# Values and scores of one half as one ranked group of products on TensorE, in a two-layer hybrid decoder step

## Chip, cores and metric

The kernel runs on one core of one Trainium2 chip, as one program. The metric is the device time of one execution in microseconds (us). TensorE is called PE here (its weight loads PEld), VectorE DVE, ScalarE ACT, GpSimd POOL; SP is the engine that issues most of the DMAs. Line numbers (L286) are those of the kernel before.

## What is computed

One inference step of a two-layer decoder trunk, for a prompt of 256 tokens and for 8 samples of 8 new tokens each, all in fp32, 320 tokens together. Each layer is

```
x += 0.5 * SwiGLU(RMSNorm(x))
x += W_out [HGRN2 | RWKV-7 | MLA](RMSNorm(x) @ W_in)
x += 0.5 * SwiGLU(RMSNorm(x))
```

The part that matters here is the MLA attention of the samples over 2048 cached positions (16 pages of 128) of a paged cache. With 8 heads and 8 new tokens a sample has 64 rows of queries:

```
s_past = einsum('bqhr,bkr->bhqk', q_lat, c_past) + einsum('bqhe,bke->bhqk', q_pe, kpe_past)
s = concat([s_past * MLA_SCALE, s_new (causal)], -1)
pr = softmax(s)
o_lat = einsum('bhqk,bkr->bqhr', pr[..., :P], c_past) + einsum('bhqk,bkr->bqhr', pr[..., P:], c)
o = einsum('bqhr,rhd->bqhd', o_lat, wuv)
```

## The kernel before

Each layer is a feed-forward block, a mixer, and a second feed-forward block. In the feed-forward blocks PE runs dense products alone: a weight block of 128x128 is split by ACT and DVE (L427, L428) into a high and a low part, and each block takes part in three products with 320 columns.

In the mixer (L555) several streams of work are interleaved. They are Python generators, and `weave` (L518) advances them by a modelled PE time `self.pe`: a stream yields how much later it wants to be called again, and the first one that is due goes on. The first stage weaves the RWKV chain (`rw`), the samples' attention (`sample`), the dense products that fill (`rw_in`, `hg_in`) and a small split stream; the second stage weaves the HGRN chain (`hg`), the prompt's attention (`prompt`), the rest of `sample` and a part of the output projection (`w_out`). This fixes the order in which instructions are written down, not yet the order on the engines: a scheduler then gives each engine, whenever it is free in a simulated time line, the ready instruction of lowest rank. The rank is the place in the written order; `tc.high_priority(offset=n)` moves it n places ahead. The streams in `self.urgent` (RWKV, HGRN, prompt) have 1000 (L530). `tc.issue_after(ins)` puts an instruction behind another one on the same engine. On the chip each engine runs its order as it stands and waits where something is missing.

`sample` (L830) takes the samples in four pairs, p = 0 to 3. Sample si of a pair (0 or 1) uses output rows 64*si to 64*si + 63, so its products have 64 stationary columns, in one half of PE's columns. The pages of a sample are taken in four chunks (ch) of 512 positions, each of two halves (hf) of 256 positions, which are two pages.

- `scores(p, ch)` (L860): for each half the transposed keys of both samples are loaded (tile `ct`, 5 buffers, one DMA a page, L874), then 3 x 2 products of 96 rows by 256 columns go into a bank of PSUM (`pa`, 2 banks; L878). Each carries on from `kt` to the next. After both halves ACT copies the bank to `S` (L884), and DVE takes the maximum (L885).
- `soft(p)` (L887) adds the scores of the new tokens and makes the negative maximum for the exponential.
- `values(p, ch, po)` (L905): the natural pages of both samples are loaded (tile `cn`, 5 buffers, one DMA a page, L917), ACT takes the exponential of the next chunk (`exps`, L903), PE transposes this chunk's `S` in four products (L925, recorded under the helper's L290), DVE copies them to `PT` (L927), and then each half has 2 pages x 2 samples of products with 256 columns (L933), which accumulate in the bank `po` (tag `pv`, one bank) over the whole pair.
- The main loop (L944) runs, for each pair, `values(p, ch)` and then `scores(p + 1, ch)` for each chunk, so the next pair's scores are made beside this pair's values. At a pair's end come the new tokens' values, the normalisation and the transposed result (L951 to L974).

All products go through `mm` (L283, recorded as L286), transposes through `tr` (L289). `ready(name, n)` (L845) gives the modelled time at which the next loads will have landed, from a pace of 1.05 us a page and from when buffers were used. `pages` (L851) reads page numbers from the table into registers of SP. Each scores product and each values product is fp32 and appears in the trace as two matmul records.

Of the kernel before, what the change touches and what calls it, by code (L numbers as in the profile page):

```python
# [26 lines left out]
RANK = 256  # L27
# [4 lines left out]
NPOOL = 160  # L32
PAGE = 128
NPAGE = 16
# [16 lines left out]
KR = 96  # L51
# [205 lines left out]
class Kern:  # L257
# [572 lines left out]
    def sample(self):  # L830
        nc, l = self.nc, self.l
        self.mark(f"sample{l}")
        idt = self.c("ident")
        cT = self.cT
        cns = self.s([64, RANK], "cns")
        ps = self.bank("pa")
# [4 lines left out]
        S, mx = {}, {}  # L841
# [3 lines left out]
        def ready(name, n):  # L845
            f = feed[name]
            f[0] = max(f[0], f[1][f[2] - 3] if f[2] > 2 else 0.0) + n * (PACE[1] if f[2] < PACE[0] else 1.05)
            f[2] += 1
            return 0, f[0] + 2.2

        def pages(i, n):  # L851

            with self.tc.issue_after(self.gat[-8].ins) if len(self.gat) >= 8 else ExitStack():
                return nc.values_load_multi_w_load_instructions(  # L854
                    self.pti[0:1, i:i + n], engines=[mybir.EngineType.SP], min_val=0, max_val=NPOOL - 1,
                    skip_runtime_bounds_check_because="a page table names pages of the pool")[1]

        ctp = self.ap["ct"].rearrange("(n p) c -> n p c", p=KR)

        def scores(p, ch):  # L860
            ps = self.bank("pa")
            for hf in range(2):
                yield ready("ct", 4)
                self.mark(f"sample{l}")
                cts = []
                for si in range(2):
                    ct = self.s([KR, 2, 3 * PAGE], "ct", 5)
                    i0 = (2 * p + si) * NPAGE + ch * 4 + hf * 2
                    rs = pages(i0, 2)

                    n = 6 + 2 * (4 * ch + 2 * hf + si)
                    with self.tc.issue_after(self.raws[n]) if p == 0 and n < len(self.raws) else ExitStack():
                        for pg, r in enumerate(rs):
                            self.gat.append(nc.sync.dma_start(ct[:, pg, :], ctp[bass.ds(r + l * NPOOL, 1)].rearrange("a p c -> p (a c)")))  # L874
                    cts.append(ct)
                for kt in range(3):
                    for si in range(2):
                        self.mm(ps[64 * si:64 * si + 64, hf * 256:hf * 256 + 256], qlat[:KR, kt, 2 * p + si],  # L878
                                cts[si][:, :, kt * PAGE:kt * PAGE + PAGE], start=kt == 0, stop=kt == 2)
                feed["ct"][1].append(self.pe)  # L880
            S[p, ch] = self.s([128, 512], "S", 5)
            if ch == 0:
                mx[p] = self.s([128, 8], "smx", 2)
            nc.scalar.copy(S[p, ch], ps)  # L884
            nc.vector.tensor_reduce(out=mx[p][:, ch:ch + 1], in_=S[p, ch], axis=AX.X, op=ALU.max)  # L885
# [16 lines left out]
            m = mx[p]  # L902
            nc.scalar.activation(S[p, ch], S[p, ch], AF.Exp, bias=m[:, 5:6], scale=MLA_SCALE, accum_out=m[:, ch:ch + 1])  # L903

        def values(p, ch, po):  # L905
            r0 = ready("cn", 4)
            cns_ = []
            rs = []
            for si in range(2):
                i = (2 * p + si) * NPAGE + ch * 4  # L910
                rs.append(pages(i, 4))
            for hf in range(2):
                for si in range(2):
                    cn = self.s([128, 2, RANK], "cn", 5)
                    for pg in range(2):
                        r = rs[si][hf * 2 + pg]
                        self.gat.append(nc.sync.dma_start(cn[:, pg, :], self.ap["cn"][l, bass.ds(r, 1)].rearrange("a p c -> p (a c)")))  # L917
                    cns_.append(cn)
            yield 0, r0[1] - 1.5
            self.mark(f"sample{l}")  # L920
            if ch < 3:
                exps(p, ch + 1)
            pt = self.bank("pa")
            for pg in range(4):
                self.tr(pt[:, pg * 128:pg * 128 + 128], S[p, ch][:, pg * 128:pg * 128 + 128], idt)  # L925
            PT = self.s([128, 512], "PT", 2)
            nc.vector.tensor_copy(PT, pt)  # L927
            yield 0, max(self.pe + 1.2, r0[1])
            for hf in range(2):
                self.mark(f"sample{l}")  # L930
                for pg in (2 * hf, 2 * hf + 1):
                    for si in range(2):
                        self.mm(po[64 * si:64 * si + 64, :RANK], PT[:, pg * 128 + 64 * si:pg * 128 + 64 * si + 64],  # L933
                                cns_[2 * hf + si][:, pg % 2, :], start=ch == 0 and pg == 0, stop=False)
                feed["cn"][1].append(self.pe)
                if hf == 0:
                    yield ready("cn", 4)

        for ch in range(4):
            yield from scores(0, ch)  # L940
        yield 0
        soft(0)
        yield 2.0
        for p in range(4):  # L944
            po = self.bank("pv")
            exps(p, 0)
            for ch in range(4):
                yield from values(p, ch, po)
                if p < 3:
                    yield from scores(p + 1, ch)  # L950
            exps(p, 4)  # L951
            nc.vector.tensor_reduce(out=mx[p][:, 6:7], in_=mx[p][:, 0:5], axis=AX.X, op=ALU.add)
            nc.vector.reciprocal(mx[p][:, 6:7], mx[p][:, 6:7])
# [581 lines left out]
```

## Time and profile before

| what | value |
|---|---|
| median of 3 runs | 1675.93 us (1675.06 to 1678.35) |
| the profiled execution, its own time | 1670.47 us |
| its span from first to last instruction | 1668.5 us |
| PE, DVE, ACT, POOL busy | 1625.2, 955.0, 716.6, 80.2 us |
| matmul records on PE | 13174 |
| granted TensorE clock, mean | 0.988 of full speed |
| DMA | 260.05 MB, 156 GB/s in the mean |

The profile is one execution, so its times are set against its own 1670.47 us. A busy time is the union of an engine's instructions; PE's records are pipelined and overlap their successors, so the time that a run of products takes is read from its start to the start of what follows it. The idle time in brackets on a timeline row lies before that row, with what ended it.

### The profile page before, as it was taken

The page shows a single profiled execution, that of the slowest core. Times are in us where ns is not written, and L with a number is a line of the kernel's source. Part 1 is how long each engine was busy: PE and PEld are TensorE (multiplying, and loading weights), DVE is VectorE, ACT ScalarE, POOL GpSimd, SP SyncE. Part 2 cuts the span into 40 slices and gives each one's busy share as a digit, 9 for nine tenths or more (in the row PEclk, how much of TensorE's full clock was granted, in tenths as well). Part 3 has the DMA queues.
Part 4 walks back from the last instruction along what each step waited for, and adds up shares of the span by engine and source line. Part 5 has one row for each costly group of instructions (what it writes and reads, how often), then busy time and mean ns, then how long its engine had stood idle before and what let it go on. Part 6 is the DMA issues. An engine that isn't in the chain of part 4 may idle for free.

```text
span 1668.5 us, 33401 instructions
## 1 busy us (share of the span) xinstructions
PE 1625.2 (97%) x13174; PEld 1449.8 (87%) x13174; DVE 955.0 (57%) x1599; ACT 716.6 (43%) x1208; POOL 80.2 (5%) x112
## 2 busy tenths in 40 slices
PE   8999999999989899999999999999999999999998
PEld 8999998777657599999999999987766676999997
DVE  7555447854446585554465554478335565755543
ACT  6444334633343364443344443346233543544432
POOL 0000000200022000000000000002000310000000
PEclk9999999999999999999999999999999999999999
DMA  8555526646564465555545555366357644555442
GB/s 282 152 150 147 149 86 170 184 143 180 155 209 138 133 209 152 152 152 149 148 146 152 152 151 148 105 175 189 109 157 208 189 134 132 159 152 150 149 148 91
DMA packets 130908, 260.05 MB, mean 156 GB/s; under 512 B 17264, under 2 KB 75952, under 8 KB 130624
## 3 DMA queue, kind: packets, MB, share of 16 engines
q1 hardware_dynamic: 119072, 237.21, 48.0%
q10 hardware_dynamic: 11648, 20.65, 4.1%
q8 instruction: 104, 1.70, 0.4%
q0 software_dynamic: 32, 0.07, 0.1%
q14 instruction: 52, 0.43, 0.1%
HBM read 253.39 MB, written 4.47 MB: 155 GB/s over the span
## 4 chain that ended last, share of the span: by engine, by line
PE 65%; DVE 2%; DMA 2%; ACT 1%; SPq 1%; issue 1%; DVEq 0%; ACTq 0%
PE pd L286 25%; PE pr L286 23%; PE pa L286 14%; PE pv L286 3%; PE pa L290 1%; DMA cn<-in_cn 1%; ACT S L903 0%; DMA ct<-in_ct 0%; DVE w L428 0%; DMA raw<-in_wm 0%; SPq L874 0%; PE pd L290 0%; SPq L917 0%; SPq L854 0%; ACT L903 0%
## 5 line engine op out<-in xcount | busy, mean ns | idle before, releaser
L428 DVE TENSOR_TENSOR w<-raw,w 128x1024 fp32r<-128x1024 f32 (+1 forms) x392 | 410.9, 1051 | 321.4 <-ACT w L427 308.9
L427 ACT CAST w<-raw 128x1024 fp32r<-128x1024 f32 (+1 forms) x392 | 354.7, 909 | 425.0 <-PE pd L286 203.1
L286 PE MATMUL pd<-xh,w 128*128 128x320 f32 x1792 | 425.2, 316 | 7.7 <-ACT w L427 6.8
L286 PEld LDWEIGHTS pd<-xh,w 128*128 128x128 f32 x1792 | 305.6, 190 | 24.2 <-issue 9.7
L286 PE MATMUL pd<-xl,w 128*128 128x320 f32 x896 | 280.1, 314 | 0.0
L286 PE MATMUL pr<-xh,w 128*128 128x320 f32 x1056 | 240.2, 310 | 0.0
L286 PE MATMUL pa<-xh,w 128*128 128x320 f32 x896 | 201.7, 309 | 0.0
L286 PEld LDWEIGHTS pr<-xh,w 128*128 128x128 f32 x1056 | 178.3, 188 | 0.5
L286 PEld LDWEIGHTS pd<-xl,w 128*128 128x128 f32 x896 | 169.7, 189 | 2.9 <-issue 0.9
L286 PE MATMUL pr<-xl,w 128*128 128x320 f32 x528 | 162.5, 309 | 0.0
L286 PE MATMUL pd<-hh,w 128*128 128x320 f32 x704 | 158.2, 309 | 0.0
L286 PE MATMUL pr<-hh,w 128*128 128x320 f32 x704 | 158.2, 309 | 0.0
L286 PEld LDWEIGHTS pa<-xh,w 128*128 128x128 f32 x896 | 151.0, 188 | 0.0
L286 PE MATMUL pa<-xl,w 128*128 128x320 f32 x448 | 137.6, 309 | 0.0
L286 PE MATMUL pa<-ct,qlat 96*64 96x256 f32 x768 | 125.1, 398 | 3.9 <-DMA ct<-in_ct 3.9
L286 PEld LDWEIGHTS pr<-hh,w 128*128 128x128 f32 x704 | 118.5, 188 | 0.0
L286 PEld LDWEIGHTS pd<-hh,w 128*128 128x128 f32 x704 | 118.5, 188 | 0.0
L286 PE MATMUL pd<-hl,w 128*128 128x320 f32 x352 | 108.8, 309 | 0.0
L286 PE MATMUL pr<-hl,w 128*128 128x320 f32 x352 | 108.8, 309 | 0.0
L286 PEld LDWEIGHTS pr<-xl,w 128*128 128x128 f32 x528 | 99.1, 188 | 0.3
L475 ACT ACTIVATE fa<-fa 128x320 f32<-128x320 f32 x88 | 41.4, 472 | 134.7 <-DVE fa L474 134.7
L286 PEld LDWEIGHTS pa<-ct,qlat 96*64 96x64 f32 x768 | 59.2, 139 | 40.5 <-issue 13.5
(381 smaller groups left out, 2011.0 us busy)
## 6 DMA issues: line engine op xcount, KB each, us to landing
raw<-in_wf SPq DMA_DIRECT2D x264, 512.0 KB, 3.6
ct<-in_ct SPq DMA_DIRECT2D x256, 144.0 KB, 2.8
cn<-in_cn SPq DMA_DIRECT2D x256, 128.0 KB, 2.4
raw<-in_wm ACTq DMA_DIRECT2D x76, 256.0 KB, 3.3
raw<-in_wm SPq DMA_DIRECT2D x52, 256.0 KB, 3.7
xT<-in_x SPq DMA_DIRECT2D x4, 320.0 KB, 6.7
wukt<-in_wukt SPq DMA_DIRECT2D x2, 576.0 KB, 6.1
S<-in_rws SPq DMA_DIRECT2D x4, 256.0 KB, 3.4
```

Of the source, the lines that this page charges most:

```text
L286: self.last = self.nc.tensor.matmul(out, w, x, start=start, stop=stop)
L290: self.nc.tensor.transpose(out, x, ident)
L427: self.cast = nc.scalar.copy(h, src).ins
L428: nc.vector.tensor_tensor(out=lo, in0=src, in1=h.bitcast(F32), op=ALU.subtract)
L475: nc.scalar.activation(a, a, AF.Silu)
```

## The change

For a half of a chunk, the products of `values` and those of `scores` for the next pair now stand together. `scores` is cut into `keys` (the loads), `scores` (the products, with a rank 2000 ahead) and `scored` (copy and maximum). `values` becomes `chunk`: it asks for the loads of both halves first, keys and values in turn; then for each half it writes the four values products (2000 ahead), page 1 before page 0 and sample 1 before sample 0, and behind them, by `issue_after` on the last of them, the six scores products, sample 1 before sample 0. The transposes of the next chunk (`turned`, 2000 ahead) are placed behind the last product of the second half; those of a pair's chunk 0 stand before its first group. Pair 0's scores and pair 3's values have no partner and stand alone, with the same rank. The time at which a half is due is the later of the two streams' times. `exps`, `soft`, the copies and the end of a pair keep their rank.

```diff
--- before.py
+++ after.py
@@ -857,27 +857,38 @@
 
         ctp = self.ap["ct"].rearrange("(n p) c -> n p c", p=KR)
 
-        def scores(p, ch):
-            ps = self.bank("pa")
-            for hf in range(2):
-                yield ready("ct", 4)
-                self.mark(f"sample{l}")
-                cts = []
-                for si in range(2):
-                    ct = self.s([KR, 2, 3 * PAGE], "ct", 5)
-                    i0 = (2 * p + si) * NPAGE + ch * 4 + hf * 2
-                    rs = pages(i0, 2)
-
-                    n = 6 + 2 * (4 * ch + 2 * hf + si)
-                    with self.tc.issue_after(self.raws[n]) if p == 0 and n < len(self.raws) else ExitStack():
-                        for pg, r in enumerate(rs):
-                            self.gat.append(nc.sync.dma_start(ct[:, pg, :], ctp[bass.ds(r + l * NPOOL, 1)].rearrange("a p c -> p (a c)")))
-                    cts.append(ct)
+        def keys(p, ch, hf):
+
+            cts = []
+            for si in range(2):
+                ct = self.s([KR, 2, 3 * PAGE], "ct", 5)
+                rs = pages((2 * p + si) * NPAGE + ch * 4 + hf * 2, 2)
+
+                n = 6 + 2 * (4 * ch + 2 * hf + si)
+                with self.tc.issue_after(self.raws[n]) if p == 0 and n < len(self.raws) else ExitStack():
+                    for pg, r in enumerate(rs):
+                        self.gat.append(nc.sync.dma_start(ct[:, pg, :], ctp[bass.ds(r + l * NPOOL, 1)].rearrange("a p c -> p (a c)")))
+                cts.append(ct)
+            return cts
+
+        def latents(p, ch, hf):
+            cns_ = []
+            for si in range(2):
+                cn = self.s([128, 2, RANK], "cn", 5)
+                for pg, r in enumerate(pages((2 * p + si) * NPAGE + ch * 4 + hf * 2, 2)):
+                    self.gat.append(nc.sync.dma_start(cn[:, pg, :], self.ap["cn"][l, bass.ds(r, 1)].rearrange("a p c -> p (a c)")))
+                cns_.append(cn)
+            return cns_
+
+        def scores(p, hf, ps, cts):
+            with self.tc.high_priority(offset=2000):
                 for kt in range(3):
-                    for si in range(2):
+                    for si in (1, 0):
                         self.mm(ps[64 * si:64 * si + 64, hf * 256:hf * 256 + 256], qlat[:KR, kt, 2 * p + si],
                                 cts[si][:, :, kt * PAGE:kt * PAGE + PAGE], start=kt == 0, stop=kt == 2)
-                feed["ct"][1].append(self.pe)
+            feed["ct"][1].append(self.pe)
+
+        def scored(p, ch, ps):
             S[p, ch] = self.s([128, 512], "S", 5)
             if ch == 0:
                 mx[p] = self.s([128, 8], "smx", 2)
@@ -902,42 +913,60 @@
             m = mx[p]
             nc.scalar.activation(S[p, ch], S[p, ch], AF.Exp, bias=m[:, 5:6], scale=MLA_SCALE, accum_out=m[:, ch:ch + 1])
 
-        def values(p, ch, po):
-            r0 = ready("cn", 4)
-            cns_ = []
-            rs = []
-            for si in range(2):
-                i = (2 * p + si) * NPAGE + ch * 4
-                rs.append(pages(i, 4))
-            for hf in range(2):
-                for si in range(2):
-                    cn = self.s([128, 2, RANK], "cn", 5)
-                    for pg in range(2):
-                        r = rs[si][hf * 2 + pg]
-                        self.gat.append(nc.sync.dma_start(cn[:, pg, :], self.ap["cn"][l, bass.ds(r, 1)].rearrange("a p c -> p (a c)")))
-                    cns_.append(cn)
-            yield 0, r0[1] - 1.5
+        def turned(p, ch):
+
+            pt = self.bank("pa")
+            with self.tc.high_priority(offset=2000):
+                for pg in range(4):
+                    self.tr(pt[:, pg * 128:pg * 128 + 128], S[p, ch][:, pg * 128:pg * 128 + 128], idt)
+            self.PT = self.s([128, 512], "PT", 2)
+            nc.vector.tensor_copy(self.PT, pt)
+
+        def chunk(p, ch, po):
+
+            both = p < 3
+            r0 = ready("cn", 4)[1]
+            if both:
+                r0 = max(r0, ready("ct", 4)[1])
+            tiles = [(keys(p + 1, ch, hf) if both else None, latents(p, ch, hf)) for hf in range(2)]
+            yield 0, r0 - 1.5
             self.mark(f"sample{l}")
             if ch < 3:
                 exps(p, ch + 1)
-            pt = self.bank("pa")
-            for pg in range(4):
-                self.tr(pt[:, pg * 128:pg * 128 + 128], S[p, ch][:, pg * 128:pg * 128 + 128], idt)
-            PT = self.s([128, 512], "PT", 2)
-            nc.vector.tensor_copy(PT, pt)
-            yield 0, max(self.pe + 1.2, r0[1])
-            for hf in range(2):
+            if ch == 0:
+                turned(p, 0)
+            yield 0, max(self.pe + 1.2 if ch == 0 else 0, r0)
+            ps = self.bank("pa") if both else None
+            PT = self.PT
+            for hf, (cts, cns_) in enumerate(tiles):
                 self.mark(f"sample{l}")
-                for pg in (2 * hf, 2 * hf + 1):
-                    for si in range(2):
-                        self.mm(po[64 * si:64 * si + 64, :RANK], PT[:, pg * 128 + 64 * si:pg * 128 + 64 * si + 64],
-                                cns_[2 * hf + si][:, pg % 2, :], start=ch == 0 and pg == 0, stop=False)
+
+                with self.tc.high_priority(offset=2000):
+                    for pg in (1, 0):
+                        for si in (1, 0):
+                            o = (2 * hf + pg) * 128 + 64 * si
+                            self.mm(po[64 * si:64 * si + 64, :RANK], PT[:, o:o + 64], cns_[si][:, pg, :],
+                                    start=ch == hf == 0 and pg == 1, stop=False)
+                if both:
+                    with self.tc.issue_after(self.last.ins):
+                        scores(p + 1, hf, ps, cts)
                 feed["cn"][1].append(self.pe)
                 if hf == 0:
-                    yield ready("cn", 4)
+                    yield 0, max(ready("cn", 4)[1], ready("ct", 4)[1] if both else 0)
+            last = self.last.ins
+            if both:
+                scored(p + 1, ch, ps)
+            if ch < 3:
+                with self.tc.issue_after(last):
+                    turned(p, ch + 1)
 
         for ch in range(4):
-            yield from scores(0, ch)
+            ps = self.bank("pa")
+            for hf in range(2):
+                yield ready("ct", 4)
+                self.mark(f"sample{l}")
+                scores(0, hf, ps, keys(0, ch, hf))
+            scored(0, ch, ps)
         yield 0
         soft(0)
         yield 2.0
@@ -945,9 +974,7 @@
             po = self.bank("pv")
             exps(p, 0)
             for ch in range(4):
-                yield from values(p, ch, po)
-                if p < 3:
-                    yield from scores(p + 1, ch)
+                yield from chunk(p, ch, po)
             exps(p, 4)
             nc.vector.tensor_reduce(out=mx[p][:, 6:7], in_=mx[p][:, 0:5], axis=AX.X, op=ALU.add)
             nc.vector.reciprocal(mx[p][:, 6:7], mx[p][:, 6:7])
```

## Rows read from the trace of the kernel before

**Rows 1.** The page, part 1: busy us, share of the span, records.

```profile
PE 1625.2 (97%) x13174; PEld 1449.8 (87%) x13174; DVE 955.0 (57%) x1599; ACT 716.6 (43%) x1208; POOL 80.2 (5%) x112
```

**Rows 2.** Windows: stretch, length, busy (instructions) by engine, granted clock, DMA share, GB/s.

```profile
294.00:580.00 286.00, 273.66 (x2950) 191.22 (x2948) 158.45 (x327) 118.58 (x264) 37.19 (x50) 0.98 0.56 165
1116.00:1410.00 294.00, 282.05 (x2990) 198.25 (x2990) 163.32 (x337) 122.31 (x269) 36.93 (x50) 0.98 0.55 161
425.00:472.00 47.00, 45.01 (x355) 28.31 (x353) 18.15 (x29) 9.07 (x22) 1.28 (x1) 0.93 0.62 180
1231.00:1300.00 69.00, 64.73 (x630) 44.49 (x630) 31.41 (x67) 31.37 (x71) 2.12 (x2) 1.00 0.64 187
```

**Rows 3.** Timeline of PE at 294 us: start, us, operation, tiles, shape, records, [idle].

```profile
294.37 2.81 PE L286 MATMUL pa<-ct,qlat 96*64 96x256 f32 x24
297.11 0.41 PE L286 MATMUL pd<-xh,w 128*128 128x320 f32 x1
297.36 0.31 PE L286 MATMUL pd<-xl,w 128*128 128x320 f32 x1
297.50 0.46 PE L286 MATMUL pd<-xh,w 128*128 128x320 f32 x2
```

**Rows 4.** Timeline of PE from 319.5 to 323.2 us.

```profile
319.53 0.31 PE L286 MATMUL pd<-xh,w 128*128 128x320 f32 x1
319.77 1.51 PE L286 MATMUL pa<-ct,qlat 96*64 96x256 f32 x10
321.21 0.41 PE L286 MATMUL pd<-xh,w 128*128 128x320 f32 x1
321.46 0.31 PE L286 MATMUL pd<-xl,w 128*128 128x320 f32 x1
...
322.58 0.65 PE L286 MATMUL pa<-ct,qlat 96*64 96x256 f32 x2
323.15 0.56 PE L286 MATMUL pd<-xh,w 128*128 128x320 f32 x2
```

**Rows 5.** Timeline of PE at 1396 us, the last such run.

```profile
1396.35 0.65 PE L286 MATMUL pv<-cn,PT 128*64 128x256 f32 x2 [1.60 <-DMA cn<-in_cn]
```

**Rows 6.** Groups by line and shape: records, busy us, mean ns, idle before, releaser.

```profile
L286 PE MATMUL pa<-ct,qlat 96*64 96x256 f32 x768 | 125.1, 398 | 3.9 <-DMA ct<-in_ct 3.9
L286 PE MATMUL pv<-cn,PT 128*64 128x256 f32 x512 | 85.7, 405 | 6.1 <-DMA cn<-in_cn 4.8 <-DVE PT L927 1.1
```

**Rows 7.** Waits of PE: waiter <- releaser: us in total, times, longest.

```profile
PE pv L286 <- DMA cn<-in_cn: 4.8, 5, 1.6
...
PE pa L286 <- DMA ct<-in_ct: 3.9, 4, 1.8
PE pr L286 <- ACT X L1124: 3.7, 2, 1.8
...
PE pr L286 <- ACT rwv L1193: 2.0, 2, 1.0
```

**Rows 8.** Timeline of SP's queue, 446 to 474 us: loads one after another.

```profile
454.82 4.54 SPq L917 DMA_DIRECT2D cn<-in_cn  x8
460.07 5.86 SPq L874 DMA_DIRECT2D ct<-in_ct  x8
```

**Rows 9.** Timelines of SP and PE: loads of cn, and the products that use them.

```profile
400.83 4.53 SPq L917 DMA_DIRECT2D cn<-in_cn  x8
...
425.06 1.03 PE L286 MATMUL pv<-cn,PT 128*64 128x256 f32 x2
```

**Rows 10.** Timeline of PE, 453 to 470 us: a chunk without and one with waits.

```profile
453.52 1.95 PE L286 MATMUL pv<-cn,PT 128*64 128x256 f32 x16
...
464.53 0.62 PE L286 MATMUL pa<-ct,qlat 96*64 96x256 f32 x2 [0.86 <-DMA ct<-in_ct]
...
466.61 1.12 PE L286 MATMUL pa<-ct,qlat 96*64 96x256 f32 x4 [1.13 <-DMA ct<-in_ct]
...
467.49 2.93 PE L286 MATMUL pv<-cn,PT 128*64 128x256 f32 x16
```

## The prediction made before the result was known

> **What bounds the kernel now.** I read the page first: PE is busy for 97% of the span [rows 1]. A busy share can hide stalls, so next I read the stretches of the two mixers (294 to 580 us and 1116 to 1410 us), the only place the change touches. PE is busy for 273.7 of 286 us and 282.1 of 294 us there; DVE stays under 60%, ACT near 42%, DMA at 0.56 [rows 2]. So 12 us per mixer are idle and the rest is PE's own queue, in order. A mixer gets shorter only if its products occupy PE for less time, or if PE waits less.
>
> Then the timeline, start to start, since ends overlap. The scores and values are fp32 products with 64 stationary columns, two records each; the sample of index 0 fills one half of the columns, index 1 the other, and two run beside each other. The run of 24 records (12 products) holds PE for 297.11 - 294.37 = 2.74 us; the run of 10 records (5 products) for 1.44 us; the run of 2 records (one product) for 0.57 us [rows 3, 4]. 2.74 - 1.44 is 1.30 for three pairs: **0.433 us a pair**, and 2.74 - 6 x 0.433 = **0.14 us for the run itself**. Five products cost three pairs (3 x 0.433 + 0.14 = 1.44) and one costs a whole pair (0.433 + 0.14 = 0.57): half a pair without its partner wastes 0.217 us. The dense neighbours pay too: inside their stretch one follows another after 0.14 to 0.15 us (297.36 to 297.50 [rows 3]), before a run after 0.24 (319.53 to 319.77), behind one after 0.25 (321.21 to 321.46 [rows 4]): 0.19 us a break.
>
> How often? From the first run at 294.37 [rows 3] to the last at 1396.35 [rows 5] I count, in the timeline, 161 unbroken runs of the 768 score and 512 value records [rows 6]; 92 have an odd number of products. Check: 320 pairs x 0.433 = 138.6, 161 x 0.14 = 22.5, 92 x 0.217 = 20.0, together 181 us; with the 8.7 us of waits for ct and cn [rows 7] 190; adding start to start gives 188 us. So some 43 us are no arithmetic.
>
> **The change part by part.**
>
> *One group per half.* Values (4 products) and the next pair's scores (6) of one half stand in one order on PE, 2000 ahead, above the 1000 of the RWKV and HGRN chains. If it works there are 24 joint groups, 8 of scores alone (pair 0) and 8 of values alone (pair 3) per mixer, 80 in all, and no odd one. PE time: 138.6 + 80 x 0.14 = 149.8 against 181: **-31 us**. The 81 breaks that go also return their neighbours' 0.19 us, less beside 64x64 products; at 0.15 that is **-12 us**. Bounds of both: if half of the 80 are still cut once, 40 x (0.14 + 0.15) = 12 us less; a gain beyond 43 has no row.
>
> *Reversed orders.* With index 1 and page 1 first, a group's first product asks for the tile loaded last, so a late load holds up its head and not its middle. By itself it adds no product: nothing.
>
> *Transposes behind the group.* The same 128 transposes and 32 copies. They need the exponentials of a pair whose scores were done before, so ACT has them early. Nothing, with a bound of 32 x 0.14 = 4 us gained where they stood in their own break, and as much lost where ACT is late.
>
> *Loads.* Keys and values of both halves are asked for ahead of the chunk, in turn on SP, in the same five buffers each, with the same 16 loads a chunk. What is queued behind a waiting load on SP is the next one, and a whole group waits for the last. SP issues eight loads of cn in 4.54 us and eight of ct in 5.86 us [rows 8], 10.4 us a chunk, while four chunks take the 47 us of 425 to 472. A faster chunk therefore has only 12% before SP sets its pace. Now most loads are early (eight cn issued from 400.83, first used at 425.06 [rows 9]), because the products wait in PE's order. Outranking takes that cover away.
>
> *The new wait at a group's head.* PE is in order: behind the head everything waits. The trace shows no group of this kind, so bounds. From below: none, and the present 8.7 us [rows 7] might go. From above: the one chunk where loads were late: idle 0.86 and 1.13 us, and the next 16 records took 2.93 us where 16 take 1.95 [rows 10], as the granted clock fell after that idleness (0.93 over the stretch around it [rows 2], so part of it at 1.2 GHz): 3.0 us a chunk, 72 for the 24 joint chunks. Between: the two stretches where loads already follow one another closely, nine chunks in 425 to 472 and 1231 to 1300 us: idle 2.0 + 4.3 us, and 0.07 x 47 = 3.3 us of clock [rows 2], 1.07 us a chunk. The joint chunks will resemble these most, being paced by the same five buffers and the same queue. 24 x 1.07 less the 9.6 already paid: **+16 us**.
>
> *The urgent chains behind a group.* A group holds PE for 5 x 0.433 + 0.14 = 2.3 us, and a step of rw or hg that comes due then waits. Dense products fill PE meanwhile; where they are missing it shows, as in the 3.7 + 2.0 us of [rows 7]. From 0 to a doubling of 5.7: **+2 us**.
>
> Sum: -31 - 12 + 16 + 2 = **-25 us**. The profiled execution took 1670.47 us (span 1668.5, 2.0 around it); the median of the runs, 1675.93, lies 5.5 us above it. With the same distance: 1670.5 - 25 + 5.5 = **1651 us**.
>
> **The rivals.** No difference under 0.2% (3.4 us) can be told from none.
>
> A: the full gain. Loads land early and stay early, since the stream also stops at each pair's end (softmax, normalisation and latent copies keep their rank). No new waits: -43 us, 1633. For it: the ten and more microseconds of cover [rows 9].
>
> B: the change does half of what it says. Where keys land after the values PE goes on with other work and the group is cut, or an odd product stays alone. Half of 43 remains and half of the new waits come: -22 + 8 + 2 = -12, 1664. For it: SP issues them in turn [rows 8]. Against: PE's order is fixed between values and scores, and the wait is put at the head.
>
> C: PE is not what paces a mixer. If SP and the buffers do, the freed time turns into idleness and the time stays, 1675. For it: SP's 10.4 of about 12 us a chunk [rows 8]. Against: outside the tight stretches PE hardly idles at all [rows 2]. The Trainium skill, Perfetto Trace Analysis, section Identifying the Most-Contended Engine, says that TensorE's headroom is to be judged by the busy share of weight loads and not of products; by it PE has a third left here (191 of 286 us [rows 2]), the saving is hidden, and the sum would be 0. The trace disagrees: in the run of 24 records PE was taken from end to end.
>
> D: slower. Every group's head waits as in [rows 10], and the clock falls with it: 3.0 us a chunk eats the 43 us from the 15th of the 24 joint chunks on; at all 24 it is 72 - 43 = +29, 1705. For it: the rank is above everything, so nothing is left between a load and its product but its landing. Against: in the tight stretches one chunk in nine went that way.
>
> **How the numbers follow.** Forecast 0.45, A 0.20, B 0.10, C 0.11, D 0.14. Faster is the first three, 0.75; the same is C, 0.11; slower is D, 0.14. The range goes from A with the old waits gone and the transposes' bound (-43 - 5, 1628) to C's edge, 1677; D beyond it and a tenth elsewhere are left out. The first three alone, 75% of the chance, lie between 1628 and 1668.
>
> **What would show it.** Right: in the timeline runs of 20 records (values, then scores) and about 80 runs in place of 161; the union of busy time of the score products falls from 125 us [rows 6] towards 100; both mixers are some 12 us shorter with the feed-forward stretches unchanged; the waits of PE for ct and cn rise from 8.7 to about 20 us. Wrong: waits over 50 us, or many stretches at a lowered clock (D); runs near 161 (B); PE's busy share falling while SP issues without a pause (C).

## The result and the profile after

The changed kernel takes **1712.2 us** in the median of 4 runs (1710.88 to 1724.37) against 1677.1 of the kernel before beside it. The medians lie 35.1 us or 2.1% apart; the ratio on record (such ratios are given from here on) is 1.024, 95% interval 1.021 to 1.028. So it is slower by 2.1 to 2.4%, outside the range given. Its profiled execution has a span of 1709.1 us, 40.6 more than before. Line numbers in rows of a changed kernel are those of that kernel.

The page, part 1, answers to [rows 1]: PE's busy time is nearly the same, its share fell from 97% to 95%.

```profile
PE 1624.2 (95%) x13174; PEld 1465.1 (86%) x13174; DVE 951.9 (56%) x1599; ACT 713.8 (42%) x1205; POOL 78.1 (5%) x112
```

Windows of the two mixers, each from its first score product to the first product of the next feed-forward block (columns as in [rows 2]); first the kernel before, then the changed one.

```profile
294.00:615.00 321.00, 308.63 (x3187) 225.31 (x3186) 188.57 (x378) 141.19 (x302) 37.19 (x50) 0.98 0.57 170
1116.00:1439.00 323.00, 311.05 (x3186) 227.09 (x3186) 187.34 (x376) 141.66 (x300) 36.93 (x50) 0.98 0.55 163
```

```profile
293.00:630.00 337.00, 305.71 (x3186) 232.20 (x3184) 187.96 (x378) 140.47 (x301) 36.02 (x50) 0.95 0.54 162
1137.00:1480.00 343.00, 310.00 (x3188) 233.60 (x3187) 185.31 (x378) 139.35 (x300) 35.87 (x48) 0.94 0.52 154
```

Such rows can be split into three terms, and all that follows uses the split. **Idle** is length less PE's busy time: 24.3 us before, 64.3 after. **Clock** is length times what the granted clock lacks to 1: 6.4 + 6.5 = 13 us before, 16.9 + 20.6 = 37 after (the clock has two digits, so give it 3 us either way). **Work** is the rest, PE's busy time as it would be at full clock: 607 before, 578 after. So the products did get cheaper by 28 us, and idleness (+40) and the lower clock that came with it (+24) took back more than twice that: +36 us in the two mixers. The clock term counts idle time as well: of 75 us at 1.2 GHz in the changed kernel's mixers 64 lay on products, of 27 before 26. On products alone the clock cost about 19 us more, and the work fell by about 23.

Where the idleness lies: the groups by line and shape (as [rows 6]) and PE's waits (as [rows 7]) of the changed kernel.

```profile
L286 PE MATMUL pa<-ct,qlat 96*64 96x256 f32 x768 | 106.2, 405 | 1.3 <-DMA ct<-in_ct 1.1
L286 PE MATMUL pv<-cn,PT 128*64 128x256 f32 x512 | 80.4, 435 | 53.2 <-DMA cn<-in_cn 49.7
```

```profile
PE pv L286 <- DMA cn<-in_cn: 49.7, 24, 3.6
...
PE pr L286 <- ACT rwv L1273: 2.0, 4, 1.1
...
PE pa L286 <- DMA ct<-in_ct: 1.1, 1, 1.1
```

PE's wait for cn grew from 4.8 us [rows 7] to 49.7. Now one such stretch on both sides: PE's groups, and below SP's queue with the loads (start, us, operation, [idle before]).

```profile
344.51 1.08 PE L286 MATMUL pv<-cn,PT 128*64 128x256 f32 x8 [1.52 <-DMA cn<-in_cn]
345.39 1.50 PE L286 MATMUL pa<-ct,qlat 96*64 96x256 f32 x12
346.82 0.38 PE L286 MATMUL pr<-bk,kkr 64*64 64x64 f32 x5
...
349.95 1.08 PE L286 MATMUL pv<-cn,PT 128*64 128x256 f32 x8
...
357.15 1.08 PE L286 MATMUL pv<-cn,PT 128*64 128x256 f32 x8 [2.29 <-DMA cn<-in_cn]
...
363.66 1.08 PE L286 MATMUL pv<-cn,PT 128*64 128x256 f32 x8 [2.95 <-DMA cn<-in_cn]
```

```profile
338.98 2.46 SPq L879 DMA_DIRECT2D cn<-in_cn  x4
342.20 2.46 SPq L870 DMA_DIRECT2D ct<-in_ct  x4
345.36 2.43 SPq L879 DMA_DIRECT2D cn<-in_cn  x4
348.56 2.46 SPq L870 DMA_DIRECT2D ct<-in_ct  x4
351.72 3.52 SPq L879 DMA_DIRECT2D cn<-in_cn  x4
356.36 2.47 SPq L870 DMA_DIRECT2D ct<-in_ct  x4
359.53 2.44 SPq L879 DMA_DIRECT2D cn<-in_cn  x4
```

The group is what the change promises: 8 + 12 records in 346.82 - 344.51 = 2.31 us, five pairs and one run. But each head starts 1.7 to 3.1 us behind the last load of cn: issued by 341.4, 347.8, 355.2 and 362.0, heads at 344.5, 350.0, 357.2 and 363.7. SP issues one load after another, 345.36 - 338.98 = 6.38 us a half (the third of these halves, with one slow issue at 351.72, took 7.8), and PE's groups come at SP's pace. It isn't so everywhere: in the whole execution SP itself waited 56.1 us for PE to free a buffer of ct and 27.0 us for one of cn, the longest 19.3 us at a pair's end. The loads of cn take no longer to land than in the kernel before. The rows give the time from issue to landing (min/median/max), first before, then changed:

```profile
DMA to landing us min/median/max: 1.9/2.4/7.6
DMA to landing us min/median/max: 1.9/2.2/6.7
```

Where PE was granted 1.2 GHz, eight such records took 1.97 us in place of 1.08, here behind a wait of 2.86 us; the second row, a window of them, has the granted clock, 0.50:

```profile
437.18 1.97 PE L286 MATMUL pv<-cn,PT 128*64 128x256 f32 x8 [2.86 <-DMA cn<-in_cn]
437.20:438.90 1.70, 1.70 (x8) 0.97 (x10) 0.00 (x0) 0.00 (x0) 0.00 (x0) 0.50 0.76 264
```

### The profile page after: what moved, and what is told of

Same layout as the page of the kernel before. It is cut to its first block, busy times and chain, and to the rows that moved or that the text cites. A ratio compares the mean times of both kernels' runs of the same rounds, so it can differ in the third digit from the quotient of the medians.

```text
span 1709.1 us, 33392 instructions
## 1 busy us (share of the span) xinstructions
PE 1624.2 (95%) x13174; PEld 1465.1 (86%) x13174; DVE 951.9 (56%) x1599; ACT 713.8 (42%) x1205; POOL 78.1 (5%) x112
## 4 chain that ended last, share of the span: by engine, by line
PE 82%; SPq 7%; DMA 4%; ACT 3%; issue 2%; DVE 2%; DVEq 0%; ACTq 0%
PE pd L286 32%; PE pr L286 29%; PE pa L286 16%; PE pv L286 3%; SPq L879 2%; SPq L854 2%; DMA cn<-in_cn 2%; SPq L870 2%; DMA raw<-in_wm 1%; PE pa L290 1%; ACT S L914 1%; DVE w L428 0%; DMA xT<-in_x 0%; PE pd L290 0%; DVE kS L451 0%
## 5 line engine op out<-in xcount | busy, mean ns | idle before, releaser
L427 ACT CAST w<-raw 128x1024 fp32r<-128x1024 f32 (+1 forms) x392 | 355.2, 909 | 423.0 <-PE pd L286 191.8
L286 PE MATMUL pv<-cn,PT 128*64 128x256 f32 x512 | 80.4, 435 | 53.2 <-DMA cn<-in_cn 49.7
L286 PE MATMUL pa<-ct,qlat 96*64 96x256 f32 x768 | 106.2, 405 | 1.3 <-DMA ct<-in_ct 1.1
L286 PEld LDWEIGHTS pv<-cn,PT 128*64 128x64 f32 x512 | 37.4, 151 | 78.2 <-DMA cn<-in_cn 33.9
```

The costliest lines, as they stand in the source:

```text
L286: self.last = self.nc.tensor.matmul(out, w, x, start=start, stop=stop)
L427: self.cast = nc.scalar.copy(h, src).ins
```

## The experiments

The theory formed from this: **SP's queue paces the ranked stream**. The rank moves groups ahead until nothing is left between a group and its loads but SP, and SP needs 12.8 us a chunk. The first rival was **the rank itself**: it holds up the urgent chains. A second one came up later: **the balance of the streams**, that is, which of samples, HGRN and prompt ends a mixer alone.

### Is it the rank?

The changed kernel without it, in three places:

```diff
-            with self.tc.high_priority(offset=2000):
+            with ExitStack():
```

> The changed kernel with the same groups in the same order, but without the rank of 2000 on products and transposes. Rank theory (a group that outranks all else is placed right behind its loads, so PE waits at its head and its clock falls): the waits of PE for cn fall from 49.7 us to under 15 us, the runs stay long (under 110 of them), and the time falls below that of before, 1640 to 1665 us. Queue theory (SP's issue of loads, with twice as many reads of page numbers for the values, paces the stream at 12.6 us a chunk whatever the rank): little changes, 1695 to 1715 us. Group theory (a run of 20 records holds up the chains that outranked it): no change, about 1710 us.

Measured: 1735.7 us, ratio 1.036 (1.033 to 1.039): slower still. PE waits 39.8 us for cn, and the end of the mixer, where HGRN and prompt are done and the samples run on alone, has idleness and a low clock (windows):

```profile
540.00:643.00 103.00, 80.26 (x484) 58.41 (x479) 39.63 (x76) 30.83 (x58) 0.00 (x0) 0.77 0.51 158
```

None of the three forecasts covers that time. So the rank is not what costs in the changed kernel, and without it PE still waits 39.8 of the 49.7 us. The other way round, the rank alone in the kernel before, on its scores, values and transposes, each as it stands there:

```diff
+                with self.tc.high_priority(offset=2000):
```

> The kernel before, with nothing but the rank of 2000 on its values, scores and transposes; loads, order and reads of page numbers as before. Rank theory: the waits for ct and cn rise from 8.7 us to 30 us or more, and the time to 1690 to 1720 us. Queue theory and group theory: neither the reads nor the groups are there, so the time is within 8 us of that of before.

Measured: 1732.2 us, 1.034 (1.030 to 1.037). This too is outside every forecast. PE hardly waits (5.9 us for ct, 4.6 for cn), but work rises by 37 us (table below): I count 172 runs instead of 161, 124 of them odd. Ranked products that come one half at a time are cut by 64x64 products of the chains between loads, and the chains pay most of it: their products took 185 us start to start in place of 156 and were left for another stream 254 times in place of 135, while the samples' products took 196 us in place of 187. So the long waits come with the fixed group, which needs every load of its half: with it they are there without the rank, and with the rank alone they are not.

### Is it SP's queue?

Page numbers are read into SP's registers by line 854. Before, a chunk of values took two reads of four numbers; the change made it four reads of two. Two kernels change that in the changed kernel. The first puts the reads of four back for cn alone. The second reads the keys' numbers by fours as well, which the kernel before did not do: four reads a joint chunk, where the kernel before has six and the changed one eight. The edit of the second:

```diff
+            rs = [pages((2 * p + si) * NPAGE + ch * 4, 4) for si in range(2)]
+            kr = [pages((2 * p + 2 + si) * NPAGE + ch * 4, 4) for si in range(2)] if both else None
...
-                rs = pages((2 * p + si) * NPAGE + ch * 4 + hf * 2, 2)
+                rs = kr[si][2 * hf:2 * hf + 2] if kr else pages((2 * p + si) * NPAGE + ch * 4 + hf * 2, 2)
...
-                for pg, r in enumerate(pages((2 * p + si) * NPAGE + ch * 4 + hf * 2, 2)):
+                for pg, r in enumerate(rs[si][2 * hf:2 * hf + 2]):
```

> The changed kernel, rank and all, but the page numbers of the values are read four at a time as before, two reads a chunk in place of four. Queue theory: SP needs some 1.4 us less a chunk, and 24 joint chunks give back 25 to 35 us, 1675 to 1690 us. Rank theory: the group follows its loads as closely as now, only the loads come a little sooner; waits for cn stay over 35 us, 1690 to 1712 us.

> The changed kernel with the page numbers of keys and values both read four at a time, four reads a joint chunk in place of eight. Queue theory: SP needs about 2.7 us less a chunk, 10 us in place of 12.6, and the time falls by 45 to 60 us to 1650 to 1667 us. Rank theory: each group still waits for the last of its loads, waits for cn over 25 us, 1680 to 1705 us.

Measured: 1698.5 us (1.014, 1.011 to 1.016) and **1682.3 us** (1.004, 1.002 to 1.006). Nothing on PE was touched, and 30 of the 35 us are gone; putting back what the change had undone gave 14 of them, reading the keys better than before another 16. Both times lie above what the queue theory gave and in the range of the rank theory. The reads by line (ns min/median/max), in the changed kernel and with four at a time:

```profile
L854 SPq TENSOR_LOAD <-pti x256: 462/472/932, 251.7 to 1430.0; - x128
```

```profile
L854 SPq TENSOR_LOAD <-pti x144: 293/300/936, 251.3 to 1355.5; - x144
```

In the second row 112 of the 144 reads are of four. With that, four loads pass in 1.91 us, and PE waits less, but still a lot:

```profile
414.82 2.06 SPq L879 DMA_DIRECT2D cn<-in_cn  x4
...
424.30 1.92 SPq L870 DMA_DIRECT2D ct<-in_ct  x4
426.40 1.91 SPq L879 DMA_DIRECT2D cn<-in_cn  x4
```

```profile
PE pv L286 <- DMA cn<-in_cn: 27.8, 19, 3.6
```

With cn alone by fours it was 27.1 us. So SP's reads account for most of the lost time, but not for all waits. In the faster kernel SP waits longer for PE to free a buffer of ct (88.9 us, 56.1 in the changed kernel); what delays the loads that are left over was not separated.

The same edit for the keys of pairs 1 to 3 in the kernel before:

```diff
+                if p and not hf:
+                    kr = [pages((2 * p + si) * NPAGE + ch * 4, 4) for si in range(2)]
...
-                    rs = pages(i0, 2)
+                    rs = kr[si][2 * hf:2 * hf + 2] if kr else pages(i0, 2)
```

> The kernel before with the page numbers of the keys of pairs 1 to 3 read four at a time, two reads a chunk in place of four; nothing else. If SP's queue paces the samples' stream in the kernel before too, 24 chunks get about 1.3 us each, 1645 to 1665 us. If its loads have cover there (they land long before they are used), no difference: 1671 to 1680 us.

Measured: 0.9996 (0.998 to 1.001), no difference. There the reads have cover; in the changed kernel they have not.

Next the order: the changed kernel asks for cn ahead of ct.

```diff
-            tiles = [(keys(p + 1, ch, hf) if both else None, latents(p, ch, hf)) for hf in range(2)]
+            tiles = [(latents(p, ch, hf), keys(p + 1, ch, hf) if both else None)[::-1] for hf in range(2)]
```

> The changed kernel with the loads of cn asked for ahead of those of ct in each half. Queue theory (SP issues without a pause, and what is issued last is late): the waits of PE move from cn (49.7 us, 24 times) to ct (1.1 us), which then has over 30 us, now between values and scores of a group; the time stays within 10 us of 1712. Rival (the pages of cn are slow to land by themselves, or wait for their buffers): the wait stays with cn, over 30 us.

Measured: 1716.3 us, 1.027 (1.023 to 1.031). The time is as expected, the split of the waits only half:

```profile
PE pa L286 <- DMA ct<-in_ct: 21.3, 19, 2.6
PE pv L286 <- DMA cn<-in_cn: 16.0, 14, 2.6
```

Over 30 us were expected for ct. It became the main wait, yet cn is late 14 times too: the whole queue is behind, not only its last entry. Then a second queue for cn, with its page reads, on ACT or on POOL:

```diff
-                for pg, r in enumerate(pages((2 * p + si) * NPAGE + ch * 4 + hf * 2, 2)):
-                    self.gat.append(nc.sync.dma_start(cn[:, pg, :], ...
+                for pg, r in enumerate(pages((2 * p + si) * NPAGE + ch * 4 + hf * 2, 2, mybir.EngineType.Pool)):
+                    self.gav.append(nc.gpsimd.dma_start(cn[:, pg, :], ...
```

> The changed kernel, rank and groups as they are, but the loads of the values and the reads of their page numbers are issued from ACT's queue in place of SP's; SP keeps the keys. Queue theory (a half's group waits for eight loads and four reads that one queue issues in a row, 6.3 us a half): SP needs about 3.2 us a half, the waits of PE for cn fall from 49.7 us to under 20 us and the time to 1640 to 1670 us, unless ACT's casts are held up behind loads that wait for a buffer. Landing theory (the scheduler puts a group where its loads land in its own time line, which is earlier than on the chip, whatever queue issues them): waits stay over 35 us, 1690 us or more.

> The same with POOL's queue in place of ACT's. Queue theory: as with ACT, 1640 to 1670 us, if POOL issues four loads a half in under 5 us. Landing theory: waits for cn stay over 35 us, 1690 us or more. If POOL takes longer to issue a load than SP, the waits for cn rise and the time goes above 1710 us; that would speak for the queue too.

Measured: ACT 1713.6 us (1.025, 1.022 to 1.028), POOL 1692.9 us (1.013, 1.009 to 1.017). On either queue the waits for ct and cn together fall from 50.8 to under 29 us, 15.0 + 13.8 and 13.9 + 9.7. On ACT nothing is won: its own work, in order, now stands behind the loads of cn, which its waits show, and PE in turn waits 7.0 us for PT and 9.1 for wuk (2.3 and 1.2 in the changed kernel). POOL has little else to do (78 us busy). Both times are in the range of the landing theory, both waits for cn in that of the queue theory. A second queue has a price of its own. With POOL the loads take longer from issue to landing, cn 5.6 us in the median for 2.2 and ct 5.7 for 3.0 (cn, then ct):

```profile
DMA to landing us min/median/max: 2.2/5.6/7.8
DMA to landing us min/median/max: 2.1/5.7/9.7
```

Where the time between issue and landing goes was not looked into. ACT's own waits, of the run with cn on ACT:

```profile
ACT rt L1291 <- DMA cn<-in_cn: 34.4, 2, 17.5
ACT S L896 <- DMA cn<-in_cn: 25.7, 4, 8.9
```

### What are the groups worth when nothing is late?

Pages of the first chunk are kept, in the changed kernel, in the kernel before (with its `scores` and `values` edited alike), and in the changed kernel without rank. These kernels leave out 240 of the 256 loads of each kind, with their reads, and compute the later chunks from the first pages; the products stay the same in number and shape.

```diff
+            if ("ct", hf) in held:
+                return held["ct", hf]
-            cts = []
+            cts = held["ct", hf] = []
...
+            if ("cn", hf) in held:
+                return held["cn", hf]
-            cns_ = []
+            cns_ = held["cn", hf] = []
```

> The changed kernel with the pages of the first chunk kept: 240 of the 256 loads of ct and as many of cn, with their page-number reads, are left out, the products stay as they are and use those tiles (the scores and values of later chunks are computed from the first pages). No group can wait for a load. Queue theory: the groups give their full worth, 31 us of products and none of the waits: 1625 to 1645, at least 20 us under the kernel before without these loads. Rival (groups, rank and the other streams cost what the products gain): no less than the kernel before without loads, 1660 or more.

> The kernel before with the same loads left out, as the base for the one above. Its waits for ct and cn are 8.7 us, which go: 1660 to 1672 by every theory. If it is well below that, loads cost the kernel before more than its waits show (by their DMA traffic beside weights).

> The changed kernel without loads and without rank 2000. Queue theory: the rank only decided how soon a group meets its late loads; without loads the groups are not late, and rank or no rank stay within 10 us of each other. Rival (without rank the samples' stream ends last and alone, whatever the loads do): over 15 us slower than with rank, and the last product of the samples comes 15 us or more behind those of HGRN and the prompt.

Measured, on one chip beside 1672.5 us of the kernel before: **1645.3** (0.983, 0.980 to 0.986), **1663.2** (0.994, 0.992 to 0.996) and 1676.5 us (1.002, 1.000 to 1.005). Without loads the change is **faster by 18 us**, just short of the 20 expected as a minimum. Windows of the mixers, changed and before:

```profile
296.00:606.00 310.00, 298.06 (x3189) 235.61 (x3187) 187.03 (x380) 140.70 (x303) 35.39 (x48) 0.97 0.20 65
1112.00:1416.00 304.00, 294.73 (x3184) 232.54 (x3183) 185.31 (x376) 135.91 (x297) 35.46 (x50) 0.98 0.19 59
```

```profile
294.00:613.00 319.00, 309.08 (x3188) 226.82 (x3188) 188.15 (x380) 141.69 (x303) 37.56 (x48) 0.97 0.20 63
1116.00:1434.00 318.00, 308.56 (x3188) 226.72 (x3187) 186.79 (x377) 140.16 (x299) 37.70 (x50) 0.97 0.18 57
```

Both are idle alike (21 and 19 us), and the changed one has 21 us less work. This splits the change in two, by the ratios: the groups are worth -18 us (0.9831 against 0.9938, 1.1%), while loads cost the kernel before 0.6% and the changed one 1.0244 - 0.9831 = 4.1%, 69 us (62 us by the medians). It says that loads are what costs, not which part of a load: issue, reads, buffers and DMA traffic all went at once.

Without loads and without rank 31 us are lost again, where the queue theory had at most 10: my theory was too narrow. The groups are cut again (114 runs, 42 odd), PE waits for the transposed S, and the samples' last product comes 40 us behind the prompt's. The rank holds a group together, and with it goes which stream ends alone.

```profile
PE pv L286 <- DVE PT L928: 13.8, 14, 2.3
```

### Does a version beat both?

All of these read page numbers four at a time; "POOL" has cn on POOL's queue. They differ in the rank of the three places:

```diff
-            with self.tc.high_priority(offset=2000):
+            with self.tc.high_priority(offset=500):
```

SP, no rank:

> The kernel of e4_four_pages_both (page numbers read four at a time for keys and values) without the rank of 2000. Without the rank the changed kernel took 1736 us, 24 us more than with it, because the samples' stream ended last and alone. If the stream is slow because of SP's queue, quicker reads help here at least as much as with the rank: 1690 to 1710 us. If it is late because of its low rank alone, the time stays at 1720 us or more. Below 1682 us the rank would be what costs.

SP, rank 500:

> Page numbers four at a time for keys and values, rank 500 in place of 2000, so that the groups stand below the chains of RWKV, HGRN and the prompt (1000) but ahead of the dense fillers. If the balance of the streams sets the end: between rank 2000 (1682) and rank 0 (1704) there is a better place, with the last product of the three streams of the second stage closer together, 1672 to 1682. If SP's queue alone sets it: no better than 1682, and the wait for cn stays at 25 to 28 us.

POOL, no rank, rank 500 and rank 2000:

> Two edits that each took time off by themselves, together: page numbers read four at a time for keys and values (1682 us), and the loads of cn issued by POOL (1693 us), and no rank 2000 (which left the samples' stream the last to end). Queue theory (the groups wait because one queue issues all sixteen loads of a chunk): each queue then carries half, about 2.7 us a chunk, the samples' products are no longer late, the wait of PE for cn falls under 10 us and the idle time of a mixer towards the 12 us of before; time at or below before, 1646 to 1672. Rival (the groups cost time because three streams must share PE, whatever the loads do): the kernel without rank stays near that with four pages and no rank, 1700, with the wait for cn low all the same.

> As the kernel with POOL's queue, four pages and no rank, with rank 500 instead. Queue theory: the wait for cn is under 10 us here as there, time 1646 to 1672, the rank moves only which stream ends last. Rival (streams sharing PE): better than without rank by as much as on SP's queue (10 to 20 us), and over 1676 both times.

> The changed kernel with both edits to the loads that each took time off by themselves: page numbers four at a time, and the loads of cn issued by POOL; the rank 2000 stays. Queue theory: SP issues about half as much, the waits for cn and ct fall to some 10 us together, and the idle time of the mixers comes near the 24 us of before; with the 31 us that the groups save that is 1640 to 1670. Rival (the groups as ranked work cost as much elsewhere as they save): between the two versions with lower rank and 1682, over 1676.

Measured, in this order: 1703.7 us (1.020, 1.017 to 1.024), 1696.3 (1.015, 1.012 to 1.019), 1698.4 (1.016, 1.013 to 1.020), 1687.3 (1.008, 1.005 to 1.011), **1682.8 (1.005, 1.004 to 1.007)**. Without rank the kernel is slower than with 2000 on either queue; rank 500 is slower on SP, and on POOL its interval overlaps that of 2000. The queue theory gave 1672 us at most for the three on POOL, and all three missed it. With POOL and rank 2000, the waits for loads fall to 18.7 us, but the time stays at 1683 and not under 1670: other waits stepped in, above all that of the last prompt heads for their softmax (wuk; w was 6.8 us before), with the samples finished 30 us earlier and few products left to fill.

```profile
PE pd L290 <- DVE wuk L809: 15.0, 2, 8.2
PE pd L286 <- ACT w L427: 12.7, 3, 7.0
PE pa L286 <- DMA ct<-in_ct: 10.8, 16, 1.5
PE pv L286 <- DMA cn<-in_cn: 7.9, 6, 3.2
```

Two attempts at that balance, both with POOL: rank 1000, and rank 2000 for joint groups alone.

```diff
-            with self.tc.high_priority(offset=2000):
+            with self.tc.high_priority(offset=2000) if p > 0 else ExitStack():
```

> POOL's queue for cn, page numbers four at a time, rank 1000 in place of 2000, so that the groups stand in the written order with the urgent chains and not ahead of them. If the balance of the streams is what is left: at 2000 the samples' last product came 30 us ahead of the prompt's, at 500 some 40 us behind; at 1000 the streams end closer together, 1665 to 1680. If cutting the groups weighs more (chains of 64x64 products come between the scores of a group): over 1683.

> POOL's queue for cn and page numbers four at a time, rank 2000 for the joint groups alone (pair 0's scores and pair 3's values and transposes keep their own rank). If the balance of the streams is what is left: the samples' last product comes later than 255 us after the mixer's start and the prompt's earlier than 285 to 293, and the time falls below 1683, 1662 to 1678. If not: 1683 or more, with the same waits for ct and cn (under 20 us).

Measured: 1686.5 us (1.007, 1.004 to 1.010) and 1686.0 (1.007, 1.004 to 1.010). Both miss. At rank 1000 the streams do end together and idleness is back at that of before, but chain products cut the groups (113 runs, 54 odd) and the work is back as well. With rank for joint groups alone the samples ended earlier, not later. No version tried beats the kernel before.

The mixers are not all of what is left. In the three kernels with POOL, fours and a rank of 2000, 1000 and 2000 for joint groups, the two mixers together last 652, 648 and 646 us, against 644 before, while the profiled executions are 21.6, 13.5 and 12.1 us longer. The rest lies outside: the first score product comes at 302, 298 and 298 us in place of 294, and the stretch between the mixers lasts 507 us in place of 501. The reason is open. (The profiled execution of the first, 1691.8 us, is its slowest of 12.)

The three terms for both mixers, worked out as above from two windows rows each; the runs of samples' products with those of an odd number counted in the timeline; and the first mixer's last products of the samples / of HGRN or prompt, from its first score product on, all in us:

| kernel | idle | clock | work | runs (odd) | streams end |
|---|---|---|---|---|---|
| before | 24 | 13 | 607 | 161 (92) | 286 / 279 |
| changed | 64 | 37 | 578 | 68 (4) | 302 / 285 |
| changed, no rank | 65 | 60 | 583 | 118 (43) | 314 / 248 |
| before, rank alone | 36 | 28 | 644 | 172 (124) | 243 / 313 |
| four pages, cn and keys | 49 | 23 | 583 | 69 (0) | 277 / 288 |
| POOL, four pages, 2000 | 49 | 23 | 580 | 70 (0) | 255 / 285 |
| POOL, four pages, 1000 | 25 | 16 | 606 | 113 (54) | 275 / 285 |
| no loads, changed | 21 | 15 | 577 | 38 (0) | 207 / 269 |
| no loads, before | 19 | 19 | 599 | 138 (76) | 282 / 280 |
| no loads, no rank | 29 | 13 | 600 | 114 (42) | 285 / 244 |

## Why the prediction was wrong

**One group per half, -31 us: right.** 161 runs became 68, odd ones 92 became 4, a group takes the 2.31 us foreseen. Start to start, the score and value products of both mixers went from 187.0 to 156.3 us with four pages a read, and without loads from 180.5 to 148.4. In the changed kernel itself 168.8, of which some 37 us ran at 1.2 GHz, against some 14 before.

**The neighbours' -12 us: not there.** The other products of the mixers (dense, chains, prompt) took 398 us start to start before, 408 in the changed kernel, and without loads 402 and 410. The breaks at the samples' runs went, but the chains' products were left more often, 135 times before and 146 after (164 without loads). That fits a break saved in one stream and paid in another, but no run separates it.

**Loads: this step failed.** It took 10.4 us a chunk for SP from the two rows of loads [rows 8], without the gaps between such rows, in which page numbers are read, and overlooked that the change turns two reads of four into four of two. The row that follows [rows 8] in the kernel before shows the gaps: from 454.82 to the next chunk's loads of cn SP took 11.66 us.

```profile
466.48 6.04 SPq L917 DMA_DIRECT2D cn<-in_cn  x8
```

That is all of the 47 / 4 = 11.75 us of the step's own four chunks: there were no 12% in hand. With the reads of two SP needs 2 x 6.38 = 12.8 us, more than PE's pace. Reading all numbers by fours took off 30 us, most of the loss, but did not turn the sign.

**The new wait at a group's head, +16 us: mis-sized, in the main for that reason.** It measured +40 idle and +24 clock, 64 us or 2.7 us for each of 24 joint chunks, next to the upper bound of 3.0 [rows 10], whose clock effect was of the right kind. The step chose the middle because in the kernel before loads rarely come that late. But its example of early loads [rows 9], 400.83 to 425.06, spans a pair's end, where the products of the new tokens run:

```profile
413.10 0.65 PE L286 MATMUL pv<-cns,PT 64*64 64x256 f32 x4
```

And its nine chunks are of a kernel in which values and scores of a half need not stand together. "Outranking takes that cover away" named the wrong cause: the rank alone left the waits for ct and cn at 10.5 us, and the group without the rank had 39.8 us for cn, and 25.4 us with its numbers read by fours. What these runs leave as the cause is the group itself: all ten products of a half stand in one order, and its head needs the last of its eight loads.

**Reversed orders and transposes, 0**: no row speaks against it. **Urgent chains, +2**: PE's wait for rwv stayed at 2.0 us [rows 7].

Of the rivals D came true: heads wait as in [rows 10], with the clock lowered. Its reason, the rank, was not the cause, and its price (1705) came near partly by luck, since it set 72 us of waits against a gain of 43, where 64 and 28 were measured. A's full gain would not have come even with every load on time: without loads the change is worth 18 us and not 43. C was half of it: SP sets the pace in the tight stretches, but the time rose, because PE's order is fixed, so PE idles at a head while dense products that could run stand behind it, and the granted clock fell with the idling. C also took a saving to be hidden while the share of weight loads is well below 1. Without loads that share was 0.71 (226.82 of 319 us), and 21 us less work still took 18 off the time. The Trainium skill (Perfetto Trace Analysis, Identifying the Most-Contended Engine) has TensorE's headroom judged by MFU, the products' rate as a share of the peak, and by the busy share of weight loads. That a shorter product brings nothing below a full share was the prediction's inference from it, and it does not hold here.

What stays open: why 27.8 us of waits remain with quick reads. More than five buffers a load would let SP run further ahead, and wasn't tried.

## What to carry over

Before tying products into a group that needs many loads at once, count everything the loads' queue must do for one such unit, register reads included, and compare that with the pace of the products; the present waits say little, since products that stand apart leave each load its own cover. Leave loads out of both kernels to learn what a new order of products is worth by itself. A rank is a lever with two ends: it holds a group together, and it shifts which stream is left alone at the end.

## What was not expected of the hardware

Reading two page numbers into SP's registers takes 472 ns in the median, four take 300: the larger read is the cheaper one. A load's issue took 1.91 / 4 = 0.48 us of SP, and a read of two with the gaps around it (6.38 - 8 x 0.48) / 4 = 0.64 us, more than one of the two loads it serves.
